# A two-layer decoder trunk: eight groups of attention exponentials turned by TensorE instead of by transfers

## The chip, the cores and the metric

One core of a Trainium2 chip runs the whole program. Its engines work from queues of their own: TensorE multiplies matrices (PE in the profile, its weight loads PEld), VectorE is DVE, ScalarE is ACT, GpSimd is POOL, and SyncE (SP) issues most transfers. The metric is the device time of one execution in microseconds; the median of the runs is compared.

## The reference, cut to what matters

`x` is 1024 rows of 1024 numbers. Layer 0 mixes tokens with dilated attention of 8 heads of width 128, in three groups of (window, dilation); layer 1 with gated linear attention; each is followed by a squared-ReLU network of width 4096. All arithmetic is float32.

```python
DILATED_GROUPS = ((128, 1), (512, 4), (2048, 16))

def dilated_attention(h, w_in, w_out):
    qkv = (h @ w_in).reshape(B, S, N_GROUPS, 3, ATTN_HEADS, HEAD_DIM)
    for g, (window, dil) in enumerate(DILATED_GROUPS):
        q = apply_rope(qkv[:, :, g, 0], cos, sin) * (HEAD_DIM ** -0.5)
        k = apply_rope(qkv[:, :, g, 1], cos, sin)
        o_g, lse_g = dilated_group_attention(q, k, v, dil, window // dil)   # softmax over a band of keys
    alpha = jax.nn.softmax(jnp.stack(lses, axis=0), axis=0)
    o = jnp.sum(alpha[..., None] * jnp.stack(outs, axis=0), axis=0)
    return o.reshape(B, S, ATTN_WIDTH) @ w_out

x = x + dilated_attention(rmsnorm(x, w0), w_in, w_out)     # layer 0
x = x + sq_relu_mlp(rmsnorm(x, w1), w_up, w_down)
x = x + gla_mixer(rmsnorm(x, w2), ...)                     # layer 1
x = x + sq_relu_mlp(rmsnorm(x, w3), w_up, w_down)
return rmsnorm(x, final_norm_w)
```

## The kernel before, in words

Every large product is cut in the manner of Strassen into seven products of half size, and each float32 operand is split into a high and a low part so that three matmuls give the product to float32's accuracy (`pe.matmul` in `Up.product`, line 599).

The stage that matters here computes queries and keys of layer 0. It is a chain of 24 **passes**, one for each head h and group g, numbered p = 3h + g (`Heads.run_head`). A pass makes the queries and keys of its own group with seven products, cut into 14 **slots** (halves of a product, six matmuls of 128x512 each, into the PSUM banks pX, pY, pV and pZ). After each slot `advance()` issues what an agenda holds for that time: `at(t, fn, rank)` puts a piece of work at slot t, and lower ranks go first. So the order of every engine's queue is written out by this agenda when the program is built; nothing is reordered later. Slot c + n below means n slots after the start of pass c; slots from 15 on lie in the pass that follows.

While pass p multiplies, `follow(p - 1)` does the attention of the group made in the pass before. In four steps j = 0 to 3 of two query blocks each: `scores` (TensorE, bank pS, L989), `soft` (mask and minimum on DVE, L1003; exponential on ACT, L1005, into the tile `pt`), a transpose of the exponentials, and `values` (TensorE, bank pO, L1069), whose rows go to DRAM (`og`). A step of the first group (g = 0) holds 4 blocks of 128x128 to be transposed (the first one 3, so 15 in all), of the second 3 (12 in all), of the third 2 (8 in all). The third group has dilation 16; the kernel lays its positions out in 8 residue classes and masks odd distances, which is the "dilation 8" of the change's name.

There are two ways to transpose:

- **By TensorE** (`turn`): one matmul against the identity for each block into a bank pP (L1016), and one ACT copy back (L1018). With its own times, `turn` at slots c + 12, 12, 16, 16 and `values` at c + 16, 16, 18, 18.
- **By transfers** (`halves` and `flip`): ACT copies the 16-bit halves of the exponentials into two planes (L1035), POOL's queue writes them to a scratch tensor in DRAM (`pscr`, L1037), SP's queue reads them back with a DMA transpose (L1048). `halves` stand at c + 11, 12, 15, 16, `flip` at c + 14, 15, 18, 19, `values` at c + 21, 21, 25, 25, that is at slots 7 and 11 of the pass that follows.

`Attention.plan` chooses. Before, the first and the third groups go by transfers and the second by TensorE: 8 first groups and 7 third groups. The groups of the last two passes have times without a `flip` (`SINGLE`, and a tuple in `tail`) and go by TensorE: the second group of head 7, done beside pass 23, and the third one, done beside the output projection.

Some other work in the same queues is spoken of below. In a pass of g = 1 or 2, the merged rows of an earlier head are weighed and added (`plan_merges`: a load of `rows` from `og`, L1209; sums on DVE, L1216 to L1234; scalings on ACT, L1229). `keep` copies a bank to SBUF on ACT (`e`, L1166), because the next product overwrites or adds to it; `column` then adds two banks on DVE (L1129), swaps the halves of the partitions by two transfers on SP (`cw`, L1130 and L1131) and applies the rotary tables four slots later (L1138 to L1146, writing `qT` and `kT`). In the last pass (23) the weights of the output projection are loaded (`W.dma`, L136, 512 KB each) and split (`W.prep`, L152 and L153), and the merged heads 0 to 3 are loaded (`ol`, L1294) and transposed (pT, L260). Then `tail()` starts the output projection (`out_proj`, pd, L214 to L216), which issues two agenda slots after each block of 12 matmuls.

Tiles come from pools; an instruction that reuses a buffer waits for its last reader. SP's transfers use eight semaphores in turn, so each one also waits until the eighth before it has landed.

Of the kernel before, what the change touches and what calls it, by code (L numbers as in the profile page):

```python
# [20 lines left out]
P = 128  # L21
# [4 lines left out]
HEADS = 8  # L26
HD = 128
AW = HEADS * HD
NG = 3
# [13 lines left out]
def hybrid_trunk(ctx, tc, x, norm_mix, norm_mlp, norm_fin, a_in, a_out, g_in, g_up, g_b, g_nw,  # L43
                 g_out, m_up, m_down, tab, msk, gmask, ident_d, out):
    nc = tc.nc
    pe, act, dve, pool, sp = nc.tensor, nc.scalar, nc.vector, nc.gpsimd, nc.sync
# [10 lines left out]
    def k4(shape, dt, name):  # L57
        return wk.tile(shape, dt, name=name, tag="k4", bufs=25)
# [53 lines left out]
    class Weights:  # L112
# [14 lines left out]
            self.slots.append(src)  # L127
            self.by.append(by)

        def dma(self, by=None):  # L130
            n = self.ndma
            if n < len(self.slots):
                self.ndma += 1
                src = self.slots[n]
                self.raws[n] = k4([P] + list(src.shape[1:]), F32, "raw")
                (by or sp).dma_start(self.raws[n], src)  # L136

        def prep(self, eng=dve):
            n = self.nprep
# [41 lines left out]
    W = Weights()  # L181
# [104 lines left out]
    class Split:  # L286
# [4 lines left out]
        @staticmethod  # L291
        def at(tiles, k):
            n = 4 // len(tiles)
            return tiles[k // n][:, k % n, :]
# [442 lines left out]
    oscr = drp.tile([S, D], F32, name="oscr")  # L737
# [241 lines left out]
    class Attention:  # L979
# [102 lines left out]
                    sp.dma_start(to.rearrange("(p r) c -> p r c", r=8)[:, 2 * j - 2:2 * j + 2, :], row)  # L1082

        def plan(self, c, points, turn, values, flip=None):
            self.by_dma = flip is not None and self.g in (0, 2)
            if flip is not None and not self.by_dma:
                turn, values = (12, 12, 16, 16), (16, 16, 18, 18)

            def get():
                self.v = load_values(self.g, self.h)  # L1090
            at(c + points[0] - 2, get)
            for j in range(4):
                t = c + points[j]
                at(t, lambda j=j: self.scores(j), 2)
                at(t + 1 + (j % 2 and points[j] == points[j - 1]), lambda j=j: self.soft(j), 2)
                if self.by_dma:
                    at(c + turn[j], lambda j=j: self.halves(j), 3)
                    at(c + flip[j], lambda j=j: self.flip(j), 3)
                else:
                    at(c + turn[j], lambda j=j: self.turn(j), 3)  # L1100
                at(c + values[j], lambda j=j: self.values(j), 4)

    class Heads(Up):
# [54 lines left out]
        def plan(self, p):  # L1158
            c = 14 * p
            st = self.st.setdefault(p, {})  # L1160
            self.behind = True

            def keep(b, name):
                def fn():
                    e = t2([P, 512], F32, name)
                    act.activation(e, st[b], AF.Copy)  # L1166
                    st[name] = e
                return fn
            at(c + 3, keep("X", "e1"), 0)
            at(c + 5, lambda: self.column(p, 0, 0, st["Y"], st["e1"]), 1)  # L1170
            at(c + 7, keep("V", "e5"), 0)
            at(c + 9, keep("X", "e2"), 0)
            at(c + 11, lambda: self.column(p, 1, 0, st["V"], st["e2"]), 1)
            at(c + 13, keep("X", "e3"), 0)
            at(c + 13, lambda: self.column(p, 1, 1, st["X"], st["e5"]), 1)
            at(c + 15, lambda: self.column(p, 0, 1, st["Z"], st["e3"]), 1)
            if p == 0:
                for s, t in ((4, 1), (6, 3), (5, 5)):
                    at(c + t, lambda s=s: self.stage(p, s), 7)
            at(c + 1, lambda: self.load(p + 1))  # L1180
            for s, t in ((0, 8), (1, 9), (2, 10), (3, 11), (4, 14), (6, 15), (5, 17)):
                at(c + t, lambda s=s: self.stage(p + 1, s), 7)
# [105 lines left out]
                reached.add((0, half))  # L1288
            at(clock[0] + 7, last)

    def ahead_h8(pairs, by=sp):

        t = h8([P, 4, 512], F32, "ol")
        by.dma_start(t, oscr[512 * pairs:512 * pairs + 512, 0:512].rearrange("(b p) c -> p b c", p=P))  # L1294
        return [t[:, 0:2, :], t[:, 2:4, :]]

    def ahead_k4(p):
# [410 lines left out]
    for i, n in enumerate(plan[:-5]):  # L1708
# [5 lines left out]
        if n == vals.STEPS - 2:  # L1714
            heads = Heads(vals.h)
# [38 lines left out]
    ol = []  # L1754
    turned = Turned(ol, x[0])
    for p in range(heads.count):
        h, g = divmod(p, NG)
        if g == 1 and h:
            plan_merges(h - 1, 14 * p)
        if p == heads.count - 1:  # L1760
            for k in range(0, KT, 2):
                add_rows(a_out, k)
            c = 14 * p
            at(c + 1, lambda: (W.dma(pool), W.dma(pool)), 0)
            at(c + 2, lambda: (W.dma(pool), W.dma(pool)), 0)
            at(c + 3, lambda: ol.extend(ahead_h8(0, pool)), 0)
            for t in (5, 6, 7, 8):
                at(c + t, lambda: W.prep(dve), 7)
            at(c + 8, lambda: turned.turn(0), 7)
            at(c + 9, lambda: (turned.load_x(0), turned.load_x(1)))  # L1770
            at(c + 11, lambda: turned.turn(1), 7)
            at(c + 17, lambda: ol.extend(ahead_h8(1)), 9)
        heads.run_head(p)
# [7 lines left out]
    def tail():  # L1781

        c = clock[0]
        heads.follow(heads.count - 1, c, ((6, 7, 8, 9), (9, 10, 11, 12), (11, 12, 13, 14)))
        load, start, finish = merges(HEADS - 1, merged)
        rows = {}
        advance()
# [605 lines left out]
    ol, turn1 = [], []  # L2393
# [81 lines left out]
```

## Time and profile before

| | |
|---|---|
| median of 3 runs | 2600.21 us (2598.14 to 2601.52) |
| the profiled execution's own time | 2598.51 us |
| its span in the profile | 2596.7 us |
| PE busy | 2574.3 us, 99% |
| PEld, DVE, ACT, POOL busy | 2142.2, 1864.0, 1298.7, 51.8 us |
| transposes on PE (pP, L1016) | 104 |
| writes to pscr on POOL, DMA transposes on SP | 68, 68 |
| DMA | mean 172 GB/s |

In an answer of the timeline each row has its start and its length in microseconds, the engine, the line, the operation, the tiles written and read, and in brackets how long the engine had been idle before it and what released it. A matmul's length (0.39 us at 128x512) is not its cost: matmuls overlap, and the cost is the distance from start to start, some 0.23 us. SPq stands for an issue in SP's queue. The profile counts a float32 product of the attention as two records (a `values` step of four blocks is x8); a transpose is one record. The output of a waits view gives the total idle time in us, the number of waits and the longest one.

### The profile page before, as it was taken

The page shows a single profiled execution, that of the slowest core. Times are in us where ns is not written, and L with a number is a line of the kernel's source. Part 1 is how long each engine was busy: PE and PEld are TensorE (multiplying, and loading weights), DVE is VectorE, ACT ScalarE, POOL GpSimd, SP SyncE. Part 2 cuts the span into 40 slices and gives each one's busy share as a digit, 9 for nine tenths or more (in the row PEclk, how much of TensorE's full clock was granted, in tenths as well). Part 3 has the DMA queues.
Part 4 walks back from the last instruction along what each step waited for, and adds up shares of the span by engine and source line. Part 5 has one row for each costly group of instructions (what it writes and reads, how often), then busy time and mean ns, then how long its engine had stood idle before and what let it go on. Part 6 is the DMA issues. An engine that isn't in the chain of part 4 may idle for free.

```text
span 2596.7 us, 33212 instructions
## 1 busy us (share of the span) xinstructions
PE 2574.3 (99%) x11985; PEld 2142.2 (82%) x11985; DVE 1864.0 (72%) x3018; ACT 1298.7 (50%) x2360; POOL 51.8 (2%) x81
## 2 busy tenths in 40 slices
PE   9999999999998999999999999999999999999998
PEld 7888888888887888888888888888888888888887
DVE  7745888888887768666657587887657866656567
ACT  6423455656655446555534345654326554553334
POOL 0000000000001000000000000000000000000000
PEclk9999999999999999999999999999999999999999
DMA  5543677777778633554775452463513544396543
GB/s 183 170 141 115 153 179 200 176 201 196 196 205 221 208 122 127 170 168 139 278 260 182 140 195 96 133 200 98 195 65 118 170 157 155 130 356 203 183 149 131
DMA packets 377911, 445.70 MB, mean 172 GB/s; under 512 B 68145, under 2 KB 240561, under 8 KB 377746
## 3 DMA queue, kind: packets, MB, share of 16 engines
q1 hardware_dynamic: 372850, 428.63, 53.5%
q0 software_dynamic: 4752, 14.68, 1.7%
q8 instruction: 94, 1.54, 0.2%
q14 instruction: 71, 0.58, 0.1%
q10 hardware_dynamic: 144, 0.26, 0.0%
HBM read 279.19 MB, written 127.60 MB: 157 GB/s over the span
## 4 chain that ended last, share of the span: by engine, by line
PE 65%; DVE 3%; ACT 1%; DMA 1%; issue 1%; SPq 0%; DVEq 0%; ACTq 0%
PE pB L1938 13%; PE pX L599 10%; PE pA L1938 10%; PE pV L599 7%; PE pY L599 3%; PE pZ L599 3%; PE pd L216 3%; PE pd L214 3%; PE pd L215 3%; PE pB L830 3%; PE pA L830 2%; PE pT L335 1%; DMA cw<-c 1%; PE pO L2236 1%; PE pU L2218 0%
## 5 line engine op out<-in xcount | busy, mean ns | idle before, releaser
L1938 PE MATMUL pB<-dh 128*128 128x512 f32 x512 | 199.4, 389 | 0.0
L1938 PE MATMUL pB<-dh,dl 128*128 128x512 f32 x512 | 199.2, 389 | 0.0
L1938 PE MATMUL pB<-dl,dh 128*128 128x512 f32 x512 | 199.2, 389 | 0.0
L223 DVE TENSOR_TENSOR dl<-sin,dh 128x1024 fp32r<-128x1024 f32 x112 | 136.8, 1221 | 42.4 <-ACT dh L220 41.8
L220 ACT ACTIVATE dh<-sin 128x1024 fp32r<-128x1024 f32 x112 | 117.8, 1052 | 88.4 <-PE pB L1938 33.4
L220 ACT ACTIVATE dh<-kept 128x1024 fp32r<-128x1024 f32 x64 | 67.9, 1061 | 183.3 <-DVE kept L1903 138.1
L599 PE MATMUL pV<-s4h,wd 128*128 128x512 f32 x448 | 150.3, 397 | 0.0
L1938 PE MATMUL pA<-dl,dh 128*128 128x512 f32 x384 | 149.4, 389 | 0.0
L1938 PE MATMUL pA<-dh,dl 128*128 128x512 f32 x384 | 149.4, 389 | 0.0
L1938 PE MATMUL pA<-dh 128*128 128x512 f32 x384 | 149.4, 389 | 0.0
L1005 ACT ACTIVATE pt<-pt,orow 128x128 f32<-128x128 f32 (+1 forms) x192 | 84.7, 443 | 75.7 <-DVE orow L1003 74.4
L1938 PEld LDWEIGHTS pB<-dh 128*128 128x128 f32 x512 | 96.2, 188 | 19.9
L1938 PEld LDWEIGHTS pB<-dl,dh 128*128 128x128 f32 x512 | 96.2, 188 | 19.9
L1938 PEld LDWEIGHTS pB<-dh,dl 128*128 128x128 f32 x512 | 96.1, 188 | 19.8
L537 DVE TENSOR_TENSOR wal<-raw,wah 128x512 fp32r<-128x512 f32 x112 | 76.2, 687 | 40.8 <-ACT wah L536 40.8
L537 DVE TENSOR_TENSOR wbl<-t,wbh 128x1024 fp32r<-128x1024 f32 x56 | 68.6, 1225 | 43.9 <-ACT wbh L536 43.8
L599 PEld LDWEIGHTS pV<-s4h,wd 128*128 128x128 f32 x448 | 84.2, 188 | 19.3 <-ACT e L1166 1.7
L608 ACT ACTIVATE c<-c 128x512 f32<-128x512 f32 x64 | 40.4, 631 | 118.6 <-DVE c L636 77.5
L223 DVE TENSOR_TENSOR dl<-kept,dh 128x1024 fp32r<-128x1024 f32 x64 | 78.4, 1225 | 24.7 <-ACT dh L220 18.7
L599 PE MATMUL pX<-s3h,wgh 128*128 128x512 f32 x224 | 89.3, 399 | 2.4 <-ACT e L1166 2.4
L599 PE MATMUL pZ<-a22h,wgh 128*128 128x512 f32 x224 | 90.1, 402 | 0.0
L599 PE MATMUL pX<-s2h,wbh 128*128 128x512 f32 x224 | 89.0, 397 | 0.0
(400 smaller groups left out, 7378.7 us busy)
## 6 DMA issues: line engine op xcount, KB each, us to landing
sin<-acts SPq DMA_DIRECT2D x112, 512.0 KB, 3.9
raw<-in_mlp_w_up_dram SPq DMA_DIRECT2D x64, 512.0 KB, 6.0
acts<-s SPq DMA_DIRECT2D x64, 512.0 KB, 3.5
raw<-in_mlp_w_down_dram SPq DMA_DIRECT2D x64, 512.0 KB, 4.8
raw<-in_attn_w_in_dram SPq DMA_DIRECT2D x98, 256.0 KB, 4.7
cw<-c SPq DMA_DIRECT2D x192, 128.0 KB, 2.8
acts<-c SPq DMA_DIRECT2D x64, 256.0 KB, 2.2
kept<-in_mlp_w_down_dram SPq DMA_DIRECT2D x32, 512.0 KB, 5.8
```

Of the source, the lines that this page charges most:

```text
L214: pe.matmul(ps, sh, mh, start=start, stop=False)
L215: pe.matmul(ps, sh, ml, start=False, stop=False)
L216: pe.matmul(ps, sl, mh, start=False, stop=stop)
L220: act.activation(hi, src, AF.Copy)
L223: dve.tensor_tensor(lo, src, hi.bitcast(F32), op=OP.subtract)
L335: pe.transpose(ps[:, k, 128 * i:128 * i + 128], xn[i][:, c:c + 128], ident)
L537: self.remain(lambda: dve.tensor_tensor(lo, src, hi.bitcast(F32), op=OP.subtract))
L599: pe.matmul(st[b], u[:, k, :], v, start=first and k + n == 0, stop=k == 3 and n == 2, skip_group_check=True)
L608: act.activation(r, r, AF.Relu)
L830: pe.matmul(self.acc[s][t], a[:, c], b[:, k, :], start=fresh and m + k + v == 0, stop=m == 1 and k == 1 and v == 2, skip_group_check=True)
L1005: act.activation(pt[:, i, :128 * n], pt[:, i, :128 * n], AF.Exp, scale=-1.0, bias=m, accum_out=self.row[:, r, HD:HD + 1])
L1938: pe.matmul(self.acc[s][t], a[:, k, c], b[:, k, :], start=fresh and m + k + v == 0, stop=m == 7 and k == 1 and v == 2, skip_group_check=True)
```

## The change

Three things change.

1. The condition in `plan`: only the first groups of heads 0 to 6 still go by transfers (7 groups). The seven third groups that went by transfers, and the first group of head 7, are turned by TensorE.
2. In the last pass the first four weight loads and the load `ol` are issued from SP's queue instead of POOL's.
3. Two times: in the passes of g = 1 but the last, `keep("X", "e2")` stands one slot earlier; and in `tail` every time of the last group is one slot later.

```diff
-        def dma(self, by=None):
+        def dma(self):
...
-                (by or sp).dma_start(self.raws[n], src)
+                sp.dma_start(self.raws[n], src)
...
         def plan(self, c, points, turn, values, flip=None):
-            self.by_dma = flip is not None and self.g in (0, 2)
+            self.by_dma = flip is not None and self.g in (0,) and self.h < HEADS - 1
             if flip is not None and not self.by_dma:
                 turn, values = (12, 12, 16, 16), (16, 16, 18, 18)
...
             at(c + 7, keep("V", "e5"), 0)
-            at(c + 9, keep("X", "e2"), 0)
+            at(c + (8 if p % NG == 1 and p < self.count - 2 else 9), keep("X", "e2"), 0)
             at(c + 11, lambda: self.column(p, 1, 0, st["V"], st["e2"]), 1)
...
-    def ahead_h8(pairs, by=sp):
+    def ahead_h8(pairs):
         t = h8([P, 4, 512], F32, "ol")
-        by.dma_start(t, oscr[512 * pairs:512 * pairs + 512, 0:512].rearrange("(b p) c -> p b c", p=P))
+        sp.dma_start(t, oscr[512 * pairs:512 * pairs + 512, 0:512].rearrange("(b p) c -> p b c", p=P))
...
-            at(c + 1, lambda: (W.dma(pool), W.dma(pool)), 0)
-            at(c + 2, lambda: (W.dma(pool), W.dma(pool)), 0)
-            at(c + 3, lambda: ol.extend(ahead_h8(0, pool)), 0)
+            at(c + 1, lambda: (W.dma(), W.dma()), 0)
+            at(c + 2, lambda: (W.dma(), W.dma()), 0)
+            at(c + 3, lambda: ol.extend(ahead_h8(0)), 0)
...
     def tail():
         c = clock[0]
-        heads.follow(heads.count - 1, c, ((6, 7, 8, 9), (9, 10, 11, 12), (11, 12, 13, 14)))
+        heads.follow(heads.count - 1, c, ((7, 8, 9, 10), (10, 11, 12, 13), (12, 13, 14, 15)))
```

How this moves instructions is shown at three places, in the order in which they stand in an engine's queue (line, operation, tile written and tiles read, shape; no time is in it).

**PE in the passes beside a third group.** At the end of slot 12 of such a pass, before:

```order
L599 MATMUL pX<-s3h,wgh 128x512
L599 MATMUL pX<-s3l,wgh 128x512
L599 MATMUL pX<-s3h,wgl 128x512
L989 MATMUL pS<-kT,qT 128x128 x4
L599 MATMUL pZ<-a22h,wgh 128x512
```

and now:

```order
L599 MATMUL pX<-s3h,wgh 128x512
L599 MATMUL pX<-s3l,wgh 128x512
L599 MATMUL pX<-s3h,wgl 128x512
L989 MATMUL pS<-kT,qT 128x128 x4
L1016 MATMUL pP<-ident,pt 128x128 x4
L599 MATMUL pZ<-a22h,wgh 128x512
```

Four transposes stand behind the scores. Four more, and the first value products, stand at slot 16, which is slot 2 of the next pass; the second value products at its slot 4. Before, both stood at its slots 7 and 11.

**PE in the last pass (23), beside the first group of head 7.** Before, the value products split slot 7 and 8, both halves of the product that adds to pX:

```order
L599 MATMUL pX<-s2l,wbh 128x512
L599 MATMUL pX<-s2h,wbl 128x512
L1069 MATMUL pO<-v,pt 128x128 x7
L599 MATMUL pX<-s2h,wbh 128x512
L599 MATMUL pX<-s2l,wbh 128x512
```

and now they stand at slot 2, behind eight transposes (seven more came at slot 12 of pass 22):

```order
L599 MATMUL pX<-a11l,wah 128x512
L599 MATMUL pX<-a11h,wal 128x512
L1016 MATMUL pP<-ident,pt 128x128 x8
L1069 MATMUL pO<-v,pt 128x128 x7
L599 MATMUL pY<-a12h,wah 128x512
```

**POOL and SP around the start of the last pass.** POOL before, where the loads of the weights (`raw`) and of `ol` stand between the writes of the last two steps of that first group:

```order
L1037 DMA pscr_93<-pt 128x2x512
L136 DMA raw<-in_attn_w_out_dram 128x1024 x2
L1037 DMA pscr_94<-pt 128x2x512
L136 DMA raw<-in_attn_w_out_dram 128x1024 x2
L1037 DMA pscr_95<-pt 128x2x512
L1294 DMA ol<-oscr 128x4x512
```

SP now, where the same loads stand between the load of `rows` and the rotary swaps `cw`:

```order
L1209 DMA rows<-og_76 128x4x390
L136 DMA raw<-in_attn_w_out_dram 128x1024 x2
L1130 DMA cw<-c 64x512
L1131 DMA cw<-c 64x512
L136 DMA raw<-in_attn_w_out_dram 128x1024 x2
L1076 DMA og_77<-orow 128x4x130
L1294 DMA ol<-oscr 128x4x512
L1076 DMA og_77<-orow 128x4x130
```

POOL's queue has none of these left. On SP, the DMA transposes that stood among these rows are gone, and the load `ol` stands behind an `og` store, which waits for the value products of slot 2.

## The prediction

> **What bounds the kernel now.** The page first:
>
> ```profile
> span 2596.7 us, 33212 instructions
> PE 2574.3 (99%) x11985; PEld 2142.2 (82%) x11985; DVE 1864.0 (72%) x3018; ACT 1298.7 (50%) x2360; POOL 51.8 (2%) x81
> ```
>
> PE is idle for 22.4 us in all. So work taken off ACT, POOL and SP is worth nothing by itself, every instruction put on PE costs its full place in PE's queue, and the only thing to win is PE's idle time. Next, who makes PE wait between 240 and 930 us, where the attention of layer 0 lies (us in total, times, longest):
>
> ```profile
> PE pO L1069 <- DMA pt<-pscr: 7.0, 5, 5.4
> PE pX L599 <- ACT e L1166: 2.4, 7, 1.1
> PE pS L989 <- DVE qT L1146: 2.2, 3, 1.7
> PE pO L1069 <- ACT pt L1018: 0.3, 1, 0.3
> ```
>
> The transfers cost PE 7.0 us, and one wait is 5.4 of it. The table by stretches says where: pass 22, the last pass (23) and the start of the output projection (length, busy us of PE, PEld, DVE, ACT, POOL, then granted clock, DMA share, GB/s):
>
> ```profile
> 792.72:816.88 24.16, 24.16 (x118) 20.44 (x117) 19.98 (x42) 13.95 (x34) 4.38 (x7) 1.00 0.77 184
> 816.88:854.11 37.23, 30.74 (x159) 26.10 (x158) 25.65 (x47) 19.27 (x45) 3.34 (x5) 0.91 0.92 251
> 854.11:863.60 9.49, 7.77 (x45) 6.33 (x44) 9.20 (x18) 3.58 (x12) 0.00 (x0) 1.00 0.96 276
> ```
>
> Pass 22, with 16 score and 16 value records, has no idle PE. The last pass has 6.5 us of it and a granted clock of 0.91. The last big wait, on PE's timeline, and the same work undisturbed in pass 22:
>
> ```profile
> 802.24 1.05 PE L1069 MATMUL pO<-v,pt 128*128 128x128 f32 x8
> 803.04 0.48 PE L599 MATMUL pX<-s2h,wbh 128*128 128x512 f32 x1
> 804.50 1.68 PE L989 MATMUL pS<-kT,qT 128*128 128x128 f32 x8
> ...
> 826.40 0.83 PE L1069 MATMUL pO<-v,pt 128*128 128x128 f32 x6
> 832.63 2.07 PE L1069 MATMUL pO<-v,pt 128*128 128x128 f32 x8 [5.41 <-DMA pt<-pscr]
> 834.93 0.63 PE L599 MATMUL pX<-s2l,wbh 128*128 128x512 f32 x1
> 835.36 0.63 PE L599 MATMUL pX<-s2h,wbl 128*128 128x512 f32 x1
> 837.07 0.82 PE L989 MATMUL pS<-kT,qT 128*128 128x128 f32 x4
> ```
>
> Undisturbed, eight value records take 0.80 us and the six matmuls behind them 1.46. In the last pass, 14 records and six matmuls should take 1.4 + 1.46 = 2.9 us; they take 837.07 - 826.40 = 10.7. The loss is 7.8: the gap of 5.41, and 2.4 more because the matmuls behind it start 0.43 us apart instead of 0.23. Why the exponentials came late stands in POOL's and SP's queues:
>
> ```profile
> 814.84 1.15 POOL L136 DMA_DIRECT2D raw<-in_attn_w_out_dram  x2
> 819.71 1.22 POOL L136 DMA_DIRECT2D raw<-in_attn_w_out_dram  x2
> 829.42 0.80 POOL L1294 DMA_DIRECT2D ol<-oscr  x1 [7.43 <-issue]
> 819.23 0.53 SPq L1209 DMA_DIRECT2D rows<-og  x1
> 821.12 10.34 SPq L1048 DMA_TRANSPOSE pt<-pscr  x2
> ```
>
> The writes to pscr share POOL's queue with weight loads of 512 KB each, and SP sits 10.34 us on two transposes that wait for them. All this belongs to the first group of head 7, which will have no transfers.
>
> **The change, part by part.** *Added: 71 transposes on PE* (7 third groups x 8, and 15). Their price, from the second groups:
>
> ```profile
> 310.52 0.82 PE L1016 MATMUL pP<-ident,pt 128*128 128x128 f32 x6
> 311.09 0.48 PE L599 MATMUL pZ<-a22h,wgh 128*128 128x512 f32 x1
> ...
> 316.66 0.82 PE L1016 MATMUL pP<-ident,pt 128*128 128x128 f32 x6
> 317.31 0.94 PE L1069 MATMUL pO<-v,pt 128*128 128x128 f32 x7
> ```
>
> Six take 0.57 us ahead of a product (0.095 each) and 0.65 ahead of values (0.108). The change has both places about equally; with a little for changing between kinds of matmul I take 0.108: **+7.7 us** (6.7 to 8.0). The value products only change places and cost the same.
>
> *Do the new transposes wait?* The last exponential of head 6's third group on ACT, and PE at slot 16, where its transposes will stand:
>
> ```profile
> 793.02 0.39 ACT L1005 ACTIVATE pt<-pt,orow 128x128 f32<-128x128 f32 x1
> 795.43 0.39 PE L599 MATMUL pY<-a12h,wah 128*128 128x512 f32 x1
> ```
>
> It is ready 795.43 - 793.41 = 2.0 us early. The second groups, which have gone this way with more blocks, show one wait on the copy back (0.3, above). I take 0 here, up to +2 (seven groups x 0.3).
>
> *Removed: 33 writes and 33 DMA transposes.* The 7.8 us of the last pass go with them: **-7.8**. The other four waits on transfers, 7.0 - 5.4 = 1.6 us, belong to first groups that stay; I keep them. With lighter traffic they could go: 0 to -1.6, and about -0.8 of restarts.
>
> *The earlier copy of e2* stands in passes of g = 1. The waits on `e` do not lie there. One of the six short ones, in pass 5 (g = 2):
>
> ```profile
> 379.41 0.39 PE L599 MATMUL pV<-s4h,wd 128*128 128x512 f32 x1
> 380.02 0.50 PE L599 MATMUL pX<-s3h,wgh 128*128 128x512 f32 x1 [0.22 <-ACT e L1166]
> ```
>
> It costs 0.61 - 0.23 = 0.4 us, six of them 2.3; there DVE and ACT also do the merge, which stays. Value 0, bound -2.3. Moved a slot, e2 only goes ahead of a weight split on ACT, which has slots to spare.
>
> *Two waits behind the big one:*
>
> ```profile
> 841.36 0.81 PE L989 MATMUL pS<-kT,qT 128*128 128x128 f32 x4
> 843.25 0.50 PE L599 MATMUL pX<-s3h,wgh 128*128 128x512 f32 x1 [1.08 <-ACT e L1166]
> 861.49 0.39 PE L216 MATMUL pd<-whi,oTl 128*128 128x512 f32 x1
> 863.61 0.68 PE L989 MATMUL pS<-kT,qT 128*128 128x128 f32 x4 [1.74 <-DVE qT L1146]
> ```
>
> The first costs 1.89 - 0.5 = 1.4. ACT's queue ahead of that e2 (weights, twelve scalings) begins once `rows` has landed; so it starts earlier, but PE comes 7.8 us earlier too. I take -0.7 (0 to -1.4). The second costs 2.12 - 0.23 = 1.9. It sits where DVE is 97% busy (9.20 of 9.49 us in the table), so DVE's queue sets it; the scores move behind six value records (0.65 us). I take **-0.6** (0 to -1.9).
>
> *The loads moved to SP.* Behind them in that queue are the rotary swaps, whose results are needed four slots (over 5 us) later, and `ol`. Times to landing between 805 and 865 us (count, KB, median us), and the place where `ol` is needed:
>
> ```profile
> rows<-og SPq DMA_DIRECT2D x2, 780.0 KB, 9.1
> ol<-oscr POOLq DMA_DIRECT2D x1, 1024.0 KB, 7.9
> 837.72 0.49 PE L260 MATMUL pT<-ident,ol 128*128 128x128 f32 x3
> ```
>
> That place is 20.8 us after the start of the last pass (816.88). Without the loss of 7.8, but with eight transposes and the values of steps 2 and 3 now ahead of it (0.9 + 1.7), it will be at 15.6. `ol` will be issued when the values of slot 2 are stored (about 5.9: two slots of 1.4, transposes 0.9, values 1.5, ACT's copy 0.6) and `rows`, issued about 1 us ahead of the pass, has landed (8.1); it lands 7.9 later, at 13.8 to 16.0. I take **+0.5** (0 to +2.5, with a landing 2 us slower).
>
> Sum: 7.7 - 7.8 - 0.7 - 0.6 + 0.5 = **-0.9 us**, against the profiled execution's 2598.5: 2597.6. That execution lies 1.7 us below the median, 2600.2 - 0.9 = 2599.3: I say **2599 us**, no change that a measurement could tell.
>
> **The rivals.** *A new wait in place of the old one (slower).* If `ol` lands as late after the start of the pass as before (829.42 + 7.9 - 816.88 = 20.4), PE stands 4.8 us at pT and runs slow for 2.4 more: 7.2 in place of 0.5, +5.8, **2606**. It decides from an issue later than 7.7 us into the pass on. For it: DMA share 0.92 in that pass, loads queued just ahead. Against it: what held `ol` back for 7.43 us lay in POOL's queue ("issue"), and five DMA transposes less share the engines here. [...]
>
> *Lighter traffic frees all (faster).* If the transfers of the third groups were what delayed the swaps and the first groups' transposes, the other waits go too: 1.6 + 0.8 + 2.3, and all of 1.4 + 1.9. Sum 7.7 - 7.8 - 3.3 - 4.7 = -8.1: **2592**. Against it: those waits lie beside first groups' own transfers and the 780 KB of `rows`, which remain.
>
> *Transposes at their full length (slower).* If each cost the length shown for one, and not the distance between starts,
>
> ```profile
> L1016 PE MATMUL pP<-ident,pt x104: 270/272/275, 310.5 to 876.5; 128*128 128x128 f32 x104
> ```
>
> 71 x 0.272 = 19.3 us, the sum is +10.7 and the time **2611**. The starts 0.095 to 0.108 apart in both places speak against it. [...]
>
> **How the numbers follow.** Forecast 0.77; late `ol` 0.11; all freed 0.10; full length 0.02. The bounds give 6.7 - 7.8 - 3.3 - 4.7 = -9.1 and 8.0 - 7.8 + 2.5 + 2 = +4.7. For eight in ten I take 2594 to 2605. With 0.2% (5.2 us) as what can be told from no change: faster needs most of the second rival, 0.09; slower the first or third, 0.11; same 0.80.
>
> **What would show it.** Right: 175 records of pP some 0.1 us apart; last pass at a clock of 1.00 and near 30 us; no wait on pscr over 1 us; passes beside third groups and their next together 0.9 us longer, without idle PE. Wrong: a wait of pT on `ol` or of pO on pP of microseconds; waits on `e` in passes of g = 2 gone; cadence of 0.43 behind transposes.

## The result

The changed kernel takes 2603.86 us (median; 2600.79 to 2605.09) where the kernel before, timed beside it, takes 2599.02 (2596.95 to 2601.52): a ratio of 1.0016, 95% interval 1.0010 to 1.0022. It is slower by 4.8 us. Forecast was 2599 and no difference.

The page of the changed kernel, span and engines:

```profile
span 2601.8 us, 33169 instructions
PE 2582.8 (99%) x12056; PEld 2149.2 (83%) x12056; DVE 1864.0 (72%) x3018; ACT 1290.5 (50%) x2359; POOL 25.5 (1%) x43
```

There are 71 more records on PE, and 8.5 us more of PE's busy time. What PE waits for between 240 and 945 us, in the form shown of before:

```profile
PE pO L1069 <- DMA pt<-pscr: 3.8, 5, 2.1
PE pS L989 <- DVE qT L1146: 1.5, 4, 1.0
PE pO L1069 <- ACT pt L1018: 1.3, 2, 0.9
PE pX L599 <- ACT e L1166: 1.1, 5, 0.2
PE pT L1277 <- DVE xs L1827: 0.7, 1, 0.7
PE pT L260 <- DMA ol<-oscr: 0.4, 1, 0.4
```

The wait of 5.4 us is gone, and yet 3.8 us of waits on transfers stand in this list. Pass 22, the last pass and the start of the output projection, in the same columns as before:

```profile
803.27:828.68 25.41, 25.41 (x128) 21.54 (x127) 19.12 (x38) 12.05 (x30) 0.00 (x0) 1.00 0.49 125
828.68:858.68 30.00, 29.53 (x168) 25.01 (x166) 26.18 (x51) 19.27 (x48) 0.00 (x0) 1.00 0.83 256
858.68:868.10 9.42, 8.43 (x52) 7.16 (x50) 9.32 (x18) 4.30 (x13) 0.00 (x0) 1.00 0.96 286
```

The last pass is 30.00 us long (37.23 before), at a clock of 1.00. So the place at which the prediction looked did about as forecast. But it starts 11.8 us later (828.68 against 816.88). PE's timeline in that pass, where the gap was, and at `ol`:

```profile
831.41 1.04 PE L1016 MATMUL pP<-ident,pt 128*128 128x128 f32 x8
832.28 1.73 PE L1069 MATMUL pO<-v,pt 128*128 128x128 f32 x14
833.76 0.48 PE L599 MATMUL pY<-a12h,wah 128*128 128x512 f32 x1
...
843.84 0.82 PE L989 MATMUL pS<-kT,qT 128*128 128x128 f32 x4
845.07 1.06 PE L260 MATMUL pT<-ident,ol 128*128 128x128 f32 x8 [0.41 <-DMA ol<-oscr]
```

Eight transposes take 0.87 us and the 14 value records behind them 1.48; nothing waits. Where the time went instead is shown by pass 17, PE's timeline:

```profile
681.96 0.83 PE L1069 MATMUL pO<-v,pt 128*128 128x128 f32 x6
684.92 1.16 PE L1069 MATMUL pO<-v,pt 128*128 128x128 f32 x8 [2.13 <-DMA pt<-pscr]
...
686.43 0.63 PE L599 MATMUL pX<-s2h,wbl 128*128 128x512 f32 x1
686.85 0.63 PE L599 MATMUL pX<-s2h,wbh 128*128 128x512 f32 x1
...
688.13 2.25 PE L989 MATMUL pS<-kT,qT 128*128 128x128 f32 x8
690.03 0.58 PE L599 MATMUL pV<-s4h,wd 128*128 128x512 f32 x1
```

This first group goes by transfers in both kernels. Now its value products wait 2.13 us, and some matmuls behind the wait start 0.43 us apart. The same place before:

```profile
675.03 0.83 PE L1069 MATMUL pO<-v,pt 128*128 128x128 f32 x6
676.16 1.16 PE L1069 MATMUL pO<-v,pt 128*128 128x128 f32 x8 [0.30 <-DMA pt<-pscr]
```

**The account.** Starts of passes are read from PE's timeline (the first record of pX<-a11h); a pass is one start to the next. For the kernel before I use the mean of its two profiles (the second one comes from the first experiments).

```
                                                     us
transposes in passes beside third groups and next   +6.7   (14 groups of four, 0.48 each)
seven transposes in pass 22                         +0.8
passes with p%3 = 2: longer (waits, restarts)       +4.7   (six passes, 165.4 in place of 160.7)
passes with p%3 = 0: longer beyond transposes       +0.4
start of the last pass to the end of the program    -7.2   (1773.1 in place of 1780.4; holds
                                                            eight transposes, +0.9)
sum                                                 +5.4   (spans: 2601.8 less 2596.45)
```

Forecast was -0.9, so the miss is 6.3 us. The third and fourth line are 5.1 of it; 0.7 is the price of the transposes (8.4 in place of 7.7), and 0.5 the last pass and what follows it (-7.2 - 0.9 = -8.1 without its transposes, in place of -8.6). The experiments ask why the waits grew, when there is less traffic than before.

### The profile page after: what moved, and what is told of

Same layout as the page of the kernel before. It is cut to its first block, busy times and chain, and to the rows that moved or that the text cites. A ratio compares the mean times of both kernels' runs of the same rounds, so it can differ in the third digit from the quotient of the medians.

```text
span 2601.8 us, 33169 instructions
## 1 busy us (share of the span) xinstructions
PE 2582.8 (99%) x12056; PEld 2149.2 (83%) x12056; DVE 1864.0 (72%) x3018; ACT 1290.5 (50%) x2359; POOL 25.5 (1%) x43
## 2 busy tenths in 40 slices
DMA packets 357270, 436.38 MB, mean 168 GB/s; under 512 B 48385, under 2 KB 220801, under 8 KB 357106
## 3 DMA queue, kind: packets, MB, share of 16 engines
q8 instruction: 94, 1.54, 0.2%
## 4 chain that ended last, share of the span: by engine, by line
PE 64%; DVE 2%; ACT 1%; issue 0%; ACTq 0%; DVEq 0%
PE pB L1938 13%; PE pX L599 10%; PE pA L1938 10%; PE pV L599 7%; PE pY L599 3%; PE pZ L599 3%; PE pd L216 3%; PE pd L214 3%; PE pd L215 3%; PE pB L830 3%; PE pA L830 2%; PE pT L335 1%; PE pO L2236 1%; PE pU L2218 0%; PE pO L2235 0%; DVE dl L815 0%
## 5 line engine op out<-in xcount | busy, mean ns | idle before, releaser
L1003 DVE CUSTOM_DVE_ANT_0 pt<-pS,masks 128x128 f32<-128x128 f32 (+1 forms) x192 | 57.7, 347 | 45.4 <-PE pS L989 45.0
```

What stands on the lines that cost most here:

```text
L1003: dve.tensor_tensor_reduce(pt[:, i, :128 * n], ps[:, i, :128 * n], masks[:, m0:m0 + 128 * n], -scale, 1e38, op0=OP.add, op1=OP.min, accum_ ...
```

## The experiments

The passes with p%3 = 2 (those that make a third group, and hold the value products of a first group) come into nearly every reading, so their lengths stand here once, summed for heads 1, 2, 3, 6 (passes 5, 8, 11, 20) and heads 4, 5 (passes 14, 17). "Packets" is explained in the fifth experiment. Times are medians; differences are against the kernel before as timed beside each. Lengths and packets come from one profiled execution of each kernel, which need not be a median one: it took 2612.9 us in k1, 2618.4 in f2 and 2598.5 in k4. "Before again" is a single run.

```
kernel                              time     diff   5,8,11,20   14,17   packets, us after the scores, heads 1-6
before                             2599.0      -     107.4      54.3    31  -  31 31 28 28
before again                       2598.0            106.3      53.4    31  -  31 31 27 28
changed                            2603.9    +4.8    108.6      56.8    28 25  25 21 21 14
e1 last first group alone          2591.8    -7.3    107.0      53.4    31  -  31  - 27 28
e2 third groups alone              2611.5   +12.4    108.9      56.5    27 25  25 21 20 14
e3 changed, e2 late                2603.0    +3.9    109.4      56.0    28 25  25 21 21 14
f1 changed, values back            2603.0    +3.8    106.8      56.2    28 26  26 21 19 15
f2 changed, flips early            2617.1   +18.0    122.1      62.5
f3 changed, values late            2603.4    +4.2    109.0      55.7    28 25  25 21 19 14
g1 e1, flips early                 2610.2   +11.1    119.6      59.9
k1 before, shifted by 50           2609.0   +10.6    112.9      58.8    21 21  22 20 19 19
k2 changed, shifted by 64          2604.5    +6.0    113.2      54.8    12 10   -  - 31 30
k3 before, loads on SP             2596.7    -1.7    106.6      53.5    31  -  30 31 27 28
k4 f1, shifted by 64               2602.5    +4.1    109.7      52.8    13 12   9 31 31 31
m1 changed, shifted by 93          2601.5    +2.7    108.4      55.0     - 31  30 28 28 25
m2 f1, shifted by 93               2601.1    +2.3    107.6      53.4     - 31  31 29 27 26
m3 e1, ol early                    2591.5    -7.3    106.4      54.1
```

(Packet times are whole microseconds, rounded down. A dash: no packet from 8 to 32 us after the scores.)

**1. The two halves of the change, each alone.**

```diff
 e1, in plan (with the loads on SP and the tail's times of the change):
-            self.by_dma = flip is not None and self.g in (0, 2)
+            self.by_dma = flip is not None and (self.g == 2 or self.g == 0 and self.h < HEADS - 1)
 e2, in plan (nothing else):
-            self.by_dma = flip is not None and self.g in (0, 2)
+            self.by_dma = flip is not None and self.g == 0
```

> Edit: the kernel before, with only the first group of head 7 turned by TensorE (15 transposes), the loads W.dma and ol of the last pass on SP, and the tail one slot later. The seven third groups go by transfers as before, and e2 stays at c + 9. Theory 'two parts': the changed kernel wins the last pass and loses in the third groups. From the start of pass 23 to the end its profile is 6.7 us shorter than the profile before, the seven transposes that lie ahead of it cost 7 x 0.12 = 0.8, so this kernel takes 5.9 us less than before (-0.23%). Rival 'chance gap': the 5.41 us gap is large only in the execution that was profiled; then the gain is below 3 us (-0.1%). Rival 'third groups lighten the last pass': the gap would also shrink through lighter traffic from the third groups, so that without them ol comes late (a wait of pT on ol of 2 us or more) and the gain is below 4 us.

> Edit: the kernel before, with only the seven third groups turned by TensorE (56 transposes). Head 7's first group still goes by transfers, the loads of the last pass stay on POOL, the tail's times and e2 stay. Theory 'two parts': 56 x 0.12 = 6.7 us for the transposes, and 3 to 4 us of new and longer waits in passes 11 to 17 as in the profile of the changed kernel, where pO waits on the copy back and on pt<-pscr: +10 us (+0.38%), and the two parts alone add up to the +4.8 of the whole. Theory 'price alone': the waits are a chance of one execution, +6.7 us (+0.26%). Rival 'the forecast's price': 56 x 0.108 = +6.0, less what the lighter traffic saves in the last pass's gap.

The last first group alone: 2591.83 us, ratio 0.9975 (0.9965 to 0.9985), a gain of 7.3 us. The third groups alone: 2611.47, ratio 1.0048 (1.0035 to 1.0060), a loss of 12.4. Together +5.1, about the +4.8 of the whole. So "two parts" holds, and the change contains a version that beats both kernels. The third groups cost 12.4 us for 56 transposes, which take 6.7; forecast was 10. In the profile of e2 the passes with p%3 = 2 are 4.6 us longer than before, and the last pass and what follows it 2.1, although its gap is 4.47 and not 5.41.

**2. The earlier copy of e2, and the kernel before a second time.**

```diff
-            at(c + (8 if p % NG == 1 and p < self.count - 2 else 9), keep("X", "e2"), 0)
+            at(c + 9, keep("X", "e2"), 0)
```

> Edit: the changed kernel with keep('X', 'e2') back at c + 9 in every pass. The forecast: no difference from the changed kernel (within 1 us), since the waits on e lie in passes of g = 2, and both profiles show them there (0.2 us each, six and five of them). Rival: in passes of g = 1 the copy of e2 collides on ACT with the copies back of the third group's transposes, which is why it was moved; then PE shows a new wait on e in up to seven passes, 0.4 us each, +2.8 us. Beside this, it is a second look at the changed kernel's waits: if the waits on the copy back in passes 12 and 15 (0.4 and 0.9) and the wait of 2.1 on pt<-pscr in pass 17 belong to the kernel, they stand again in the same passes; if they are chance, other passes show them, and other lengths.

> The kernel before, unchanged, for a second profile. Theory 'two parts': the gap of 5.41 us on pt<-pscr in the last pass stands again, at over 4 us, with the long hold of ol in POOL's queue, and the waits of the other passes are under 0.6 each. Rival 'chance gap': it is under 3 us, or another pass has a gap of this size.

With e2 late the time is 2603.0 (ratio 1.0016, 1.0007 to 1.0025): no difference from the changed kernel, as forecast. Its profile shows waits of 1.8 and 2.1 us in passes 14 and 17. The waits on transfers are thus not a chance of one execution, though pass 14 had 0.32 in the first profile. In the second profile of the kernel before the big gap stands again:

```profile
824.82 0.83 PE L1069 MATMUL pO<-v,pt 128*128 128x128 f32 x6
831.44 0.79 PE L1069 MATMUL pO<-v,pt 128*128 128x128 f32 x2 [5.80 <-DMA pt<-pscr]
```

**3. The spacing.** A step of a first group is a chain: scores, exponentials, copies, writes to pscr, DMA transposes, value products. Its two ends on PE and its last issue on SP, first group of head 5, first before, then changed:

```profile
653.14 1.68 PE L989 MATMUL pS<-kT,qT 128*128 128x128 f32 x8
669.26 1.89 SPq L1048 DMA_TRANSPOSE pt<-pscr  x1
```

```profile
660.98 1.68 PE L989 MATMUL pS<-kT,qT 128*128 128x128 f32 x8
676.55 1.67 SPq L1048 DMA_TRANSPOSE pt<-pscr  x1
```

The value products come at 675.03 and at 681.96 (above). So PE is there 21.89 us after the scores in the one and 20.98 in the other, 0.9 less, and the transposes are issued 0.55 earlier (16.12 and 15.57). The chain has lost 0.35 us of slack, in each of six passes. The reason lies in the third group: its second value products (eight records, 0.8 us) stood at slot 11 of that pass, between these scores and these value products, and the change moved them to slot 4, ahead of both. The test puts them back:

```diff
                 turn, values = (12, 12, 16, 16), (16, 16, 18, 18)
+                if self.g == 2:
+                    values = (16, 16, 25, 25)
```

> Edit: the changed kernel, with the second value products of the seven third groups back at c + 25 (slot 11 of the next pass, where they stood before); the first ones stay at c + 16. The number of instructions is the same. The theory 'spacing': in the changed kernel those eight records (0.8 us) no longer stand between the scores of the first group (slot 8 of that pass) and its value products (slot 7 of the next), so PE is at the value products 20.99 us after the scores in place of 21.89, while the DMA transposes are issued only 0.55 us earlier (15.57 in place of 16.12); 0.35 us of slack less, and the waits on pt<-pscr in passes with p%3 = 2 grow by 4.7 us in all. With the products back, the two distances are 21.9 and 16.1 again, those passes lose about 15 us over their undisturbed length as in both profiles before (not 20), and the time is 4.7 us under the changed kernel: 2599. Rival 'traffic': the transposes land late (7 to 8 us and not 6 to 7) because of what the third groups' stores and loads now do to the DMA engines, whatever PE's distance; then passes 14 and 17 show waits of 1 to 2 us again and the time stays at 2602 to 2604.

2602.96 us (ratio 1.0014, 1.0006 to 1.0023): the time did not fall as forecast. The table says why. The distances are 21.89 and 16.1 again; passes 5, 8, 11 and 20 are back from 108.6 to 106.8, the length before. Passes 14 and 17 are not (56.2), and the passes with p%3 = 0 became 1.8 us longer, where PE now waits for the copy back of second groups (1.9 us in two waits). So the spacing is one cause, worth about 2 us, but not the whole: waits of 1.7 and 0.9 us stand in passes 14 and 17, and the time is where the rival 'traffic' had put it.

**4. Three ways to give the transfers more time.**

```diff
-        POINTS = (8, 8, 12, 12), (11, 12, 15, 16), (21, 21, 25, 25), (14, 15, 18, 19)
 f2, and g1 on top of e1:
+        POINTS = (8, 8, 12, 12), (11, 12, 15, 16), (21, 21, 25, 25), (14, 14, 18, 19)
 f3:
+        POINTS = (8, 8, 12, 12), (11, 12, 15, 16), (22, 22, 25, 25), (14, 15, 18, 19)
```

> Edit: the changed kernel, with the DMA transposes of the second step of every first group one slot earlier (c + 14 and not c + 15), so that they stand ahead of the load rows (780 KB) in SP's queue. Both theories, 'spacing' and 'traffic', say that the waits on pt<-pscr in the passes with p%3 = 2 go, if the load rows is what the transposes land behind: -4.7 us for what the change added, and -2 to -3 for the short waits (0.3 to 0.6 and their restarts, six passes) that the kernel before has too: 2596 to 2597. If the writes to pscr are what is late, the transposes only sit longer in SP's queue and the time stays at 2602 to 2604.

> Edit: the kernel with head 7's first group alone turned by TensorE (2591.8 us), with the DMA transposes of the second step one slot earlier as well. If they land behind the load rows, the waits of 0.2 to 0.5 us on pt<-pscr go with their restarts: -2 to -3 us, 2589 to 2590. If not, 2592.

> Edit: the changed kernel, with the first value products of the first groups one slot later (c + 22 and not c + 21), all else as it was: PE gets 1.37 us more slack and the DMA queues keep their order. 'Spacing': no wait on pt<-pscr is left but for landings over 8 us; -5 to -7 us, 2597 to 2599. 'Traffic' with landings of 8.3 us and more in passes 14 and 17: 0.5 to 1 us of each of these two is left, 2599 to 2600. If the waits are not what the third groups cost, the time stays at 2603 to 2604.

The main forecast of all three missed. f2 takes 2617.11 (ratio 1.0058, 1.0044 to 1.0071), g1 2610.21 (1.0042, 1.0029 to 1.0054), f3 2603.38 (1.0016, 1.0007 to 1.0025). In none of them is a wait on pt<-pscr left, and each has another in its place. The waits of f2, and the first row of f3's:

```profile
PE pS L989 <- DVE qT L1146: 14.3, 7, 3.5
PE pV L599 <- ACT e L1166: 3.3, 4, 0.9
```

```profile
PE pS L989 <- DVE qT L1146: 9.5, 9, 1.9
```

In f2, SP stands 3.83 us on three transposes, and `rows` and the rotary swaps `cw` go out 1.3 to 1.4 us later; the scores of the next step need what comes of these swaps. In f3 nothing is issued later, and the scores still wait 9.5 us. In its pass 17 the second swap lands 22.1 us after the scores of the pass before, and the transposes at 23.0. They land within 1 us of each other, so putting off PE's use of the one shows the wait for the other. The time of f3 is that of its last case ("the waits are not what the third groups cost"), but its trace does not bear that case out: the waits went and others took their place.

**5. The instruction fetch.** Passes 14 and 17 stay long whatever the spacing. The DMA queues between the issue of the second transpose and the value products that wait for it, pass 17, before and then changed (packets, MB, share of 16 engines; the last row the median us to landing of the transposes issued there whose landing is known):

```profile
q1 hardware_dynamic: 2129, 1.49, 82.9%
q0 software_dynamic: 160, 0.52, 20.0%
...
pt<-pscr SPq DMA_TRANSPOSE x2, 5.9
```

```profile
q1 hardware_dynamic: 2994, 1.92, 88.9%
q0 software_dynamic: 160, 0.52, 16.1%
q8 instruction: 1, 0.02, 0.8%
q14 instruction: 1, 0.01, 0.2%
...
pt<-pscr SPq DMA_TRANSPOSE x2, 8.3
```

The transpose that PE waits for, the first of the two, lands 6.9 us after its issue before and 8.3 us now (the 5.9 is the mean of 6.9 and 4.9). The changed kernel has two packets there that the one before has not, of queues that the page calls instruction. q8 has 94 packets and 1.54 MB in the whole program, on the page of the changed kernel:

```profile
q8 instruction: 94, 1.54, 0.2%
```

That is 16.4 KB a packet, and 24112 weight loads and matmuls of PE over 94 packets are 257 each; from these numbers I estimate 64 bytes an instruction. I take it as PE's instruction stream, one packet every 128 matmuls; the median count of matmuls between two packets in the trace is 127 to 128. Each is counted with about 1 us of one DMA engine's time (0.8% of 16 engines over 8.35 us). If that is what they are, where the packets fall follows from the number of matmuls ahead, and 71 more shift them. The test leaves the attention alone and adds cheap matmuls at the program's start:

```diff
+    def tiny(n):
+        for _ in range(n):
+            pe.matmul(idle[0:32, 0:32], warm[:, 0:32], warm[:, 0:32], start=True, stop=True)
...
-    run_in(6)
+    tiny(55)       # k1, on the kernel before; 69 in k2 and k4, 98 in m1 and m2
+    run_in(1)
```

> Edit: the kernel before, with six of the warm-up matmuls at the very start replaced by 55 tiny ones (32x32) and one: 50 matmuls more in PE's instruction stream and none of them near layer 0's attention. The theory 'fetch': PE's instructions are read by a DMA queue of their own (q8 in the profile: 94 packets of 16 KB, one per some 128 matmuls, about 1 us each on one DMA engine). A packet that falls between the issue of the second DMA transpose of a first group (15.6 to 16.1 us after the group's scores) and its landing (22 to 23) delays it by 1 to 2 us. In the kernel before the packets fall 27 to 31 us after the scores in five of the six passes, so the waits are short by luck; 50 matmuls earlier they fall at 17 to 21, and the waits on pt<-pscr in these passes grow from 0.2-0.5 to 1-2 us each: the passes with p%3 = 2 become 4 to 8 us longer in all, though nothing of the third groups is changed: 2603 to 2607. Theories without the fetch: only the start moves (50 tiny matmuls, up to 3 us less the six replaced ones): the passes keep their lengths.

2609.00 us, ratio 1.0042 (1.0030 to 1.0055), +10.6 us, more than forecast. The tiny matmuls cost nothing (the first pass starts at 246.76 us in both). The packets fall 19 to 22 us after the scores in all six passes (28 to 31 in five of them before), and PE's first waits are now

```profile
PE pO L1069 <- DMA pt<-pscr: 18.4, 7, 6.9
```

Six of the seven are 1.4 to 2.2 us and lie in the six passes, which are 11.0 us longer; another 4.0 us of this profile lie in the last pass and behind it. So the kernel before is sensitive to this too and had its packets in harmless places. That q8 moves with PE's matmuls, and that PE waits longer for the transposes where it falls, is shown; in pass 17 two transposes land 6.6 us after their issue in the median, 5.9 before. It is not so each time: in pass 14 of the changed kernel's first profile a packet fell at 21 and the wait was 0.32. How 1 us of one DMA engine becomes 1 to 2 us of waiting is not shown. The second instruction queue, q14, is not the cause: none of its packets falls between 11 and 25 us in the six passes of k1.

> Edit: the changed kernel, with six warm-up matmuls at the start replaced by 69 tiny ones and one: 64 matmuls more, half a packet's distance. 'Fetch': the packets that fall 18 to 22 us after the scores in passes 14 and 17 fall about 14 us earlier, at 5 to 8, and so do the others (12 to 14), all ahead of the transposes' issue; the waits of 1 to 2 us in passes 14 and 17 go, those two passes together are 53.8 to 54.3 us long as in the kernel before (56.0 to 56.8 in the three profiles with the third groups on TensorE), -2 to -2.5 us, part of which a wait on the copy back in passes 9 to 15 may take again: 2601 to 2602.5. 'Spacing' alone, or 'traffic': passes 14 and 17 stay at 56, 2603 to 2604.

> Edit: the changed kernel with both: the second value products of the third groups back at c + 25, and 64 matmuls more at the start. If the 4.7 us that the passes with p%3 = 2 lost come from the spacing (passes 5, 8, 11, 20: 2.0 us) and from the fetch (passes 14 and 17: 2.4 us), these passes come down to a loss of 15 to 16 us over their undisturbed length, as before. The waits on the copy back in passes with p%3 = 0, which grew by 1.9 us when the spacing was mended alone, decide how much of it is kept: 2599.5 to 2602.

k2: 2604.45 (ratio 1.0020, 1.0012 to 1.0029), a miss. Passes 14 and 17 are shorter, though not as much as forecast (54.8, not 56.8), but passes 5 and 8 grew to 29.5 and 29.2. Their packets went to 10 and 12 us after the scores, which I had called harmless. There they fall among the transposes of the first step (issued from 11.7 to 14.2 us after the scores in pass 17 before); SP issues `rows` 0.7 to 0.9 us later, and what stands behind it in its queue follows. k4: 2602.50 (1.0012, 1.0003 to 1.0021), 0.5 above its forecast; the passes whose packet went to 31 are short (14 and 17: 52.8).

All profiles in which the first value products stand at c + 21 give 84 passes of this kind (p%3 = 2, heads 1 to 6). Where no packet of q8 falls from 8 to 23 us after the scores (61 passes), PE waits 1.0 us at most for these transposes, 0.34 in the median. With a packet at 19 to 22 us the wait is 0.9 to 2.2 in 13 of 14 passes, and with one at 9 to 13 us it is 0.9 to 2.6 in 4 of 5. At 14 and 15 us it is 0.4 at most, but all four of these are pass 20. The last two runs put the packets outside 9 to 22 us in all six passes:

> Edit: the changed kernel, with six warm-up matmuls at the start replaced by 98 tiny ones and one: 93 matmuls more. The packets of PE's instruction fetch should fall 8 us later in relation to the scores of the first groups (128 - 93 = 35 matmuls later): at 36, 33, 33, 29, 29 and 22 us for heads 1 to 6, where 28, 25, 25, 21, 18-21 and 14 are seen in the changed kernel. 'Fetch': passes 14 and 17 together are 53.8 to 54.8 long (56.0 to 56.8 before the shift), the waits on pt<-pscr are all under 0.7, and only pass 20 may show a longer one; passes 5, 8 and 11 stay as they are through the spacing: 2601 to 2602. If a third cause is there, passes 14 and 17 stay above 56 and the time at 2603 to 2604.5.

> Edit: the changed kernel with the second value products of the third groups back at c + 25 and 93 matmuls more at the start. Both causes mended: the passes with p%3 = 2 lose 15 to 16 us over their undisturbed length, as before (19.9 in the changed kernel), no wait on pt<-pscr over 0.6: 2599 to 2601, what the 71 transposes cost and the last pass saves, plus what the waits on the copy back in passes with p%3 = 0 take (0 to 2).

m1: 2601.53 (ratio 1.0009, 1.0000 to 1.0017); passes 14 and 17 fall to 55.0 (0.2 over the forecast) and no wait on pt<-pscr is over 0.7:

```profile
PE pO L1069 <- DMA pt<-pscr: 2.7, 6, 0.7
PE pT L260 <- DMA ol<-oscr: 1.3, 1, 1.3
```

m2: 2601.06 (1.0011, 1.0003 to 1.0020). With both causes mended, the passes with p%3 = 2 take 161.0 us, as in the kernel before (160.7). The four kernels make a square: 165.4 us in the changed kernel, 162.9 in f1, 163.5 in m1, 161.0 in m2. So the spacing is worth 2.5 us with the shift and without it, and the fetch 1.9. Each is one profile; the five profiles of kernels that leave these passes as they were (before twice, e1, k3, m3) lie between 159.7 and 161.7, so either size is good to about 1 us. Time and interval alone would not part m1 from the changed kernel (intervals 1.0000 to 1.0017 and 1.0010 to 1.0022); the passes do. In m2 passes with p%3 = 0 are still 1.7 us longer than before beyond their transposes; what delays the copies back there is not settled.

**6. Which half of the last pass's edit closes the gap.**

```diff
-            at(c + 1, lambda: (W.dma(pool), W.dma(pool)), 0)
-            at(c + 2, lambda: (W.dma(pool), W.dma(pool)), 0)
-            at(c + 3, lambda: ol.extend(ahead_h8(0, pool)), 0)
+            at(c + 1, lambda: (W.dma(), W.dma()), 0)
+            at(c + 2, lambda: (W.dma(), W.dma()), 0)
+            at(c + 3, lambda: ol.extend(ahead_h8(0)), 0)
```

> Edit: the kernel before, with only the four weight loads and ol of the last pass moved from POOL's queue to SP's; all transposes stay as they were. If POOL's queue, in which the writes to pscr stand among four loads of 512 KB, is what made the gap of 5.4 us, the gap shrinks to that of the other passes (0.2 to 0.6) and the time falls by 6 to 8 us without a single transpose more on PE: 2591 to 2593. If the traffic of these 2 MB and of rows (780 KB) is what delays the writes and the transposes, whichever queue issues them, the gap stays at 3 us or more: 2596 to 2600, and the transposes on TensorE are what removed it.

2596.74, ratio 0.9994 (0.9985 to 1.0003): between the two forecasts, not told from no change. The last pass:

```profile
825.40 0.83 PE L1069 MATMUL pO<-v,pt 128*128 128x128 f32 x6
828.79 1.29 PE L1069 MATMUL pO<-v,pt 128*128 128x128 f32 x8 [2.57 <-DMA pt<-pscr]
...
834.68 1.09 PE L260 MATMUL pT<-ident,ol 128*128 128x128 f32 x8 [1.10 <-DMA ol<-oscr]
```

The gap is 2.57 and not 5.41, and `ol` comes late as well. The pass is 34.5 us long in place of 37.2, but from its end to the next product cut in seven it takes 109.8 us in place of 107.2 (107.7 in the second profile before): the gain of the pass is lost behind it. Nor did the late transpose wait for a write, as the prediction and the first case above have it. The write that it reads (pscr_93) landed 0.9 us into the pass, and SP began to issue the transpose at 4.2. SP was at this one issue for 6.57 us, and the transpose landed at 15.7. In k3 the write landed at 0.3, the issue began at 5.3 and took 2.93 us, and the landing came at 12.9. What moved are the loads: POOL issued the first one 2.0 us ahead of the pass, SP 2.5 us into it, and the two transposes that SP issued around the start of the pass landed 2.4 and 3.0 us after their issue in place of 8.1 and 6.7. The gap shrank by 2.8 us with loads that came from another queue and were also issued later; this run cannot tell the queue from the time of the loads. Of the versions run, only those with the transposes on TensorE have no gap.

**7. The last first group alone, with `ol` earlier.** e1 with `ol` loaded ahead of the second pair of weights:

```diff
-            at(c + 2, lambda: (W.dma(), W.dma()), 0)
-            at(c + 3, lambda: ol.extend(ahead_h8(0)), 0)
+            at(c + 2, lambda: ol.extend(ahead_h8(0)), 0)
+            at(c + 3, lambda: (W.dma(), W.dma()), 0)
```

> Edit: the kernel with head 7's first group alone turned by TensorE (2591.8 us), with ol loaded at slot 2 of the last pass, ahead of the second pair of weight loads. pT waited 1.5 us on ol there. If ol lands earlier by the place of the two weight loads (1 MB, 2 to 3 us), the wait goes: -1.5 us, 2590.3. If rows and the weights ahead of it set its landing, or the weights' splits come late instead, no difference: 2591.8.

2591.47, ratio 0.9976 (0.9966 to 0.9986); PE's wait on `ol` is gone from the list of waits, and the time is that of e1. In the profiles the last pass is 0.9 us shorter than in e1 and the rest of the program behind it 1.5 longer; the waits on qT are 1.7 us in all, 0.6 in e1. e1 and this version are the fastest of all, and the times do not part them.

## Why the prediction was wrong

- **The step that failed** is "the other four waits on transfers ... belong to first groups that stay; I keep them", value 0, bounds 0 to -1.6. They grew, and with their restarts and what follows them cost 4.7 us. I asked only whether less traffic would shorten them. I did not ask what the moved value products had stood between: they were part of the time that PE gave to another group's transfers (2.5 us in the square of the fifth experiment), and the other part came with the count of PE's instructions (1.9 us), which I had not thought of at all. The bound of +2 on new waits was set for the new transposes, where hardly anything came.
- **The price of a transpose** was 0.12 us in groups of four and 0.11 in groups of seven and eight: 8.4 us for 71, where 7.7 was taken and 6.7 to 8.0 given as bounds: a second term that was too small. That a short group carries more of the change of kind is my reading, and no run tests it. The third rival (0.272 each) is out. No cadence of 0.43 stands behind transposes: the matmuls behind them start 0.32 us apart at most, and in layer 0's attention the granted clock is below 1.00 only from 686.3 to 689.7 us, where none stands.
- **The last pass** was right: -7.8, -0.7, -0.6 and +0.5, that is -8.6 without transposes, where the account gives -8.1. Length 30.00 us and clock 1.00 were forecast. `ol` was needed 15.8 us into the pass (843.84 + 0.65 - 828.68, four scores taking 0.65 as from 837.07 to 837.72 before) and came 0.6 later, 0.4 beyond the landing that was given. The wait on `e` went whole (1.4, where 0.7 was taken). The wait in the tail fell from 1.74 to 0.99, but the 0.6 is not seen in the time: from the start of the output projection to the end of the program it is 1743.1 us, and 1742.6 and 1743.1 in the two profiles before. The reason given for the gap, that the transposes wait for writes that stand among loads, is wrong for the transpose that ended it (sixth experiment).
- **e2** cost and gave nothing, as taken, and the new transposes do not wait for exponentials. 175 records of pP were seen.
- **The rivals.** "Late `ol`" came as 0.4 us, not 4.8. "Lighter traffic frees all" is refuted: less was moved (436.38 MB against 445.70 in the program), and the waits on the transfers that stay grew from 1.6 to 3.8 us.
- **The range**, 2594 to 2605, held the time, by luck: its upper part stood for waits at pP and a late `ol`, and other waits filled it. The change in sign did not come from any rival that I named; "no wait on pscr over 1 us" was the sign that I gave for it, and it was broken at 2.13.

## What to carry to other kernels

When work leaves a stretch of the critical engine, ask whose transfers were hidden behind it: eight records moved seven slots took 0.35 us of slack from a chain that they have nothing to do with. A change that holds several parts is worth timing apart, since here one part won 7.3 us and the other lost 12.4. And where PE's instruction count changes ahead of a stretch that waits on transfers (here with 83 to 89% of 16 DMA engines' time on q1), the same kernel with a few dozen cheap matmuls at its start can show how much of a difference is only where the packets of q8 fall: 50 of them made 10.6 us here.

## What was not expected of the hardware

- The page counts a queue named instruction in the time of the same 16 DMA engines that move the data: 94 packets of 16.4 KB, one every 127 to 128 matmuls in the median. 50 cheap matmuls at the start of this program, far from anything that waits, made it 10.6 us slower; with them the packets moved into the bad stretch of six passes (from 28 to 31 us after the scores to 19 to 22), which took 11.0 us more in the profile.
- A wait of 2.13 us in pass 17 was followed, 1.5 us after its end, by some 3.6 us of matmuls at half rate (0.43 apart in place of 0.23, with a granted clock of 0.54 from 686.43 to 690.03); waits of 2.08 and 2.23 in the same kind of pass of e3 and e2 had none. In k1 a wait of 2.17 us in pass 14 was followed in the same way, and waits of 2.17 and 2.20 in its passes 8 and 17 were not. Why is open.
